# Two accumulators of the first half's projections in one two-bank PSUM tile, in a hybrid HGRN2 and stick-breaking decoder step

## The chip, the core and the metric

One core of one Trainium2 chip runs the whole step as a single program. The metric is the device time of one execution in microseconds (us), the median of several executions. TensorE (PE in the profile) multiplies matrices and writes its sums into PSUM, an accumulator memory of eight banks, each 128 partitions by 512 float32 values. ScalarE (ACT) and VectorE (DVE) read PSUM and do the elementwise work, GpSimd (POOL) gathers cache pages, and the DMA queue of SyncE (SP) brings the weights.

## What is computed

Two layers act on 1024 prompt tokens and on 8 sample tokens, of width 1024. Layer 0 mixes tokens with a gated linear recurrence (HGRN2) beside an attention over 256 memory tokens. After layer 0 one shared K and V is projected. Layer 1 mixes with stick-breaking attention over that K and V, again beside the memory attention. Each layer ends in a SwiGLU block of width 2816. Cut to what matters here:

```python
def swiglu(h, w_gu, w_down):
    gate, up = jnp.split(h @ w_gu, 2, axis=-1)
    return (jax.nn.silu(gate) * up) @ w_down
...
    for l in range(DEPTH):
        g = g_norm[l]
        hn = rmsnorm(h, g[0])
        if l < N_A:
            mix, S = a_mixer(hn, w_in_a[l], lbs[l], hg_norm[l], mem_k[l], mem_v[l], w_o[l], hg_s0[l])
...
        else:
            mix = b_mixer(hn, w_in_b[l - N_A], sb_bias[l - N_A], k_all, v_all, q_pos, k_pos,
                          mem_k[l], mem_v[l], w_o[l])
        h = h + rmsnorm(mix, g[1])
        h = h + rmsnorm(swiglu(rmsnorm(h, g[2]), w_gu[l], w_down[l]), g[3])
        if l == N_A - 1:
            sb_k, sb_v = jnp.split(rmsnorm(h, g_kv) @ w_kv, 2, axis=-1)
```

## The kernel before

**Two halves.** The tokens are cut in two groups that share all weights. Group 0, the first half, is 512 prompt tokens. Group 1, the second half, is the other 512 and the 8 sample tokens, 520 columns. [...]

**A projection.** Every product with a weight matrix goes through `proj` (lines 256 to 268). It makes one accumulator: 128 output features by the group's columns, summed over `nk` blocks of 128 inputs. `split_w` (line 240) loads each 128x512 piece of weights, and ACT (line 250) and DVE (line 251) split it into a high and a low float32r part, so that each block takes three matmuls: high by high, high by low, low by high. With 8 blocks a first-half accumulator has 24 matmuls of 512 columns; in the down projection of the SwiGLU block it has 15 or 12. The split weights stand in five buffers (`wspl`), two of which one 8-block projection fills.

**The accumulator's tile.** `proj` takes a tile `[P, 2, 512]` from the pool `mmp`, which has two buffers, four banks in all. A second-half accumulator fills both banks of its tile. A first-half accumulator writes bank 0 and leaves bank 1 unused (`pv`, line 234, reads `ps[:, 0, :G]`). So two accumulators exist at a time in either half, and the third can start when the reader of the first is done. The other PSUM pools (`smp` with three banks, `nsp` with one) are not touched.

**Readers of the accumulators.** `silu` (line 274) reads its accumulator three times: ACT takes the absolute value (line 277), exponential and logarithm follow (278, 279), DVE takes a minimum and subtracts (280), ACT exponentiates (281), and DVE multiplies by the accumulator (283). The last reader is line 283. In the SwiGLU block (`ffn.part`, line 462) a slice of 128 features is a gate accumulator read by `silu` and an up accumulator read by one DVE multiply (line 472). After 4 or 5 slices the down projection adds 8 accumulators to the residual with one DVE addition each (line 401; a copy on ACT, line 399, in the first part and in `out_proj.mm`, line 411). `heads2` (762), `v_proj` (780), `gate_proj` (791) and `kv_proj` (991) loop over 4 heads, one accumulator per head, read by `silu` or by one ACT copy (942, 785, 799, 997).

**The order.** The stages are generators. `drain` runs them to their end and `weave` (line 222) takes turns between them, so that the recurrence or attention of one half stands beside the SwiGLU parts of the other (lines 1142 to 1193). This sets only the priorities: a scheduler orders the instructions of each engine when the program is built, by its own estimate of when each can run, hands out the buffers of the pools, and writes the semaphores. On the chip each engine then runs its list strictly in that order, and an instruction that waits holds all behind it on its engine.

Of the kernel before, what the change touches and what calls it, by code (L numbers as in the profile page):

```python
# [8 lines left out]
F32 = mybir.dt.float32  # L9
# [8 lines left out]
P = 128  # L18
# [4 lines left out]
def tile_decoder(  # L23
# [8 lines left out]
    ND = D // P  # L32
    NB = x_sample.shape[0]
    NM = mem_prompt.shape[1]
    H = 4
    DFF = w_down.shape[1]
# [3 lines left out]
    G = 512  # L40
    NG = [G, G + NB]
    PW = [G, (G + NB) // 2]
    NPC = [1, 2]
# [3 lines left out]
    def pool(name, bufs, **kw):  # L47
        return ctx.enter_context(tc.tile_pool(name=name, bufs=bufs, **kw))
# [13 lines left out]
    mmp = pool("mmp", 2, space=PSUM)  # L62
# [5 lines left out]
    def nm(s):  # L68
        uid[0] += 1
        return f"{s}_{uid[0]}"  # L70
# [13 lines left out]
    def A(dt=F32):  # L84
        return apool.tile([P, 2, WID], dt, tag="a", name=nm("a"))
# [15 lines left out]
    def C():  # L101
        return cpool.tile([P, 2, 512], F32, tag="c", name=nm("c"))
# [4 lines left out]
    def small(shape, dt=F32, tag="sm", bufs=None):  # L107
        return spool.tile(shape, dt, tag=tag, name=nm(tag), bufs=bufs)
# [39 lines left out]
    for lv in range(7):  # L148
        m = 1 << lv
# [82 lines left out]


    def pv(ps, g):
        return ps[:, 0, :G] if g == 0 else ps[:, :, : PW[1]]

    def sv(ap, g):
        return ap[:, :G] if g == 0 else ap.rearrange("p (a n) -> p a n", a=2)
# [1 line left out]
    def split_w(W, k0, nk, m0):  # L240
        out = []
        for a in range(0, nk, 4):
            n = min(4, nk - a)
            raw = wraw.tile([P, 4, P], F32, tag="w", name=nm("w"))
            nc.sync.dma_start(
                raw[:, :n, :],
                W[(k0 + a) * P : (k0 + a + n) * P, m0 : m0 + P].rearrange("(k p) m -> p k m", p=P),
            )
            ws = wspl.tile([P, 2, 4, P], F32R, tag="ws", name=nm("ws"))
            nc.scalar.copy(ws[:, 0, :n, :], raw[:, :n, :])  # L250
            nc.vector.tensor_sub(ws[:, 1, :n, :], raw[:, :n, :], ws[:, 0, :n, :].bitcast(F32))  # L251
            for i in range(n):
                out.append((ws[:, 0, i, :], ws[:, 1, i, :]))
        return out

    def proj(g, W, k0, nk, m0, xt):
        w = split_w(W, k0, nk, m0)
        ps = mmp.tile([P, 2, 512], F32, tag="mm", name=nm("mm"))
        for k in range(nk):
            wh, wl = w[k]  # L260
            for wi, (wt, xi) in enumerate(((wh, 0), (wh, 1), (wl, 0))):
                for a in range(NPC[g]):
                    o = a * PW[g]
                    nc.tensor.matmul(  # L264
                        ps[:, a, : PW[g]], wt, xt[k][:, xi, o : o + PW[g]],
                        start=(k == 0 and wi == 0), stop=(k == nk - 1 and wi == 2),
                    )
        return ps
# [136 lines left out]
    class out_proj:  # L405


        def __init__(self, g, l, store, last=False):
            self.g, self.l, self.store, self.x, self.last = g, l, store, [], last

        def mm(self, xo, m0=0, m1=ND):
            g = self.g
            if m0 == 0:
                self.R = R_from(self.store)
                self.acc = small([P, WID], tag="st", bufs=3)
            for m in range(m0, m1):
                ps = proj(g, w_o[self.l], 0, ND, m * P, xo)
                evac_raw(g, self.R, ps, m, self.acc, True, True)
                yield

# [36 lines left out]
    class ffn:  # L457
# [4 lines left out]
        def part(self, pi):  # L462
            g, l = self.g, self.l
            n = NG[g]
            f0, nf = PARTS[pi]
            last = pi == len(PARTS) - 1
            mids = []
            for j in range(nf):
                pg = proj(g, w_gu[l], 0, ND, (f0 + j) * P, self.xt)
                sg = silu(None, pg, g)  # L470
                pu = proj(g, w_gu[l], 0, ND, DFF + (f0 + j) * P, self.xt)
                nc.vector.tensor_mul(sv(sg, g), sv(sg, g), pv(pu, g))  # L472
                mt = M(F32R)
                split_to((mt[:, 0, :n], mt[:, 1, :n]), sg[:, :n])
                mids.append(mt)
                yield
            if pi == 0:
                self.R = R_one()
            if last:
                self.acc = small([P, WID], tag="st", bufs=3)  # L480
            for m in range(ND):
                ps = proj(g, w_down[l], f0, nf, m * P, mids)
                evac_raw(g, self.R, ps, m, self.acc, pi == 0, last)
                if last and self.rows:
                    nc.scalar.activation(
                        self.R[m][:, :n], self.R[m][:, :n], AF.Copy, scale=gcol(l, 3, m)
                    )
                    if m == 3:
                        self.first_half()
                if m % 2:  # L490
                    yield
# [268 lines left out]
    carry = const.tile([P, H, P], F32, name="carry")  # L760

    def heads2(g, W, m0, xt, evac, alloc, out):
        for h in range(H):
            if h % 2 == 0:
                out.append(alloc())
            ps = proj(g, W, 0, ND, m0 + h * P, xt)
            evac(out[-1][:, h % 2, :], ps, g)
            yield

# [8 lines left out]
            )  # L778

    def v_proj(g, W, m0, xt, vt, vs):  # L780
        vt.extend((C(), C()) if g else (A(), A()))
        for h in range(H):
            ps = proj(g, W, 0, ND, m0 + h * P, xt)
            t = T()
            nc.scalar.copy(sv(t, g), pv(ps, g))
            to_token(t, vt, h)
            if g:
                nc.vector.tensor_copy(vs[:, h, :], t[:, G : G + NB])
            yield

    def gate_proj(g, W, xt, Ft, Kt):
        n = NG[g]
        for h in range(H):
            if h % 2 == 0:
                Ft.append(A())
                Kt.append(A())
            ps = proj(g, W, 0, ND, 4 * P + h * P, xt)
            f = T()
            nc.scalar.copy(sv(f, g), pv(ps, g))
            e = T()  # L800
            nc.vector.scalar_tensor_tensor(e[:, :n], f[:, :n], -1.0, f[:, :n], op0=ALU.mult, op1=ALU.min)
            nc.scalar.activation(e[:, :n], e[:, :n], AF.Exp)
            nc.scalar.activation(e[:, :n], e[:, :n], AF.Ln, bias=1.0)
            nc.vector.scalar_tensor_tensor(e[:, :n], f[:, :n], 0.0, e[:, :n], op0=ALU.min, op1=ALU.subtract)
            nc.vector.tensor_sub(f[:, :n], e[:, :n], f[:, :n])
            Fd = Ft[-1][:, h % 2, :n]
            Kd = Kt[-1][:, h % 2, :n]
            nc.scalar.activation(Fd, e[:, :n], AF.Exp)
            nc.scalar.activation(Kd, f[:, :n], AF.Exp)
            nc.vector.tensor_scalar(Fd, Fd, oml[:, h : h + 1], lb[:, h : h + 1], op0=ALU.mult, op1=ALU.add)  # L810
            nc.vector.tensor_scalar(Kd, Kd, oml[:, h : h + 1], None, op0=ALU.mult)
            yield
# [176 lines left out]


    def kv_proj(g, xt):
        ks = small([P, 2, H, NB], tag="ks", bufs=1) if g else None
        for j, (out, scr) in enumerate(((sbk_prompt, ksc), (sbv_prompt, vsc))):
            for h in range(H):
                ps = proj(g, w_kv, 0, ND, (j * H + h) * P, xt)
                t = T()
                nc.scalar.copy(sv(t, g), pv(ps, g))
                if g:
                    nc.vector.tensor_copy(ks[:, j, h, :], t[:, G : G + NB])
                pt = S()  # L1000
                for c in range(CH):
                    nc.tensor.transpose(pt[:, c * P : (c + 1) * P], t[:, c * P : (c + 1) * P], ident)
                tok = T()
                nc.vector.tensor_copy(tok[:, :G], pt)
                nc.sync.dma_start(
                    out[0, g * G : (g + 1) * G, h, :].rearrange("(c p) d -> p c d", p=P),
                    tok[:, :G].rearrange("p (c d) -> p c d", d=P),
                )
                nc.sync.dma_start(scr[h][:, g, :], t[:, :G] if j == 0 else tok[:, :G])
                yield  # L1010
        if g:
            for j, dst in enumerate((sbk_sample, sbv_sample)):
                pt = S()
                for h in range(H):
                    nc.tensor.transpose(pt[:NB, h * P : (h + 1) * P], ks[:, j, h, :], ident)
                t = T()
                nc.vector.tensor_copy(t[:NB, :512], pt[:NB, :])
                nc.sync.dma_start(dst.rearrange("b o h d -> (b o) (h d)"), t[:NB, :512])
            yield
# [136 lines left out]
    f0 = ffn(0, 0, o0.x)  # L1156
# [28 lines left out]
    f0 = ffn(0, 1, o0.x)  # L1185
# [40 lines left out]
```

## Time and profile before

| what | us |
|---|---|
| median of three runs | 2559.78 (2555.36 to 2562.91) |
| the profiled execution, its own time | 2560.6 |
| its span in the profile | 2558.9 |
| PE busy in the span | 2525.4 |
| DVE busy | 1556.9 |
| ACT busy | 1218.0 |
| granted PE clock, mean | 0.992 |

By stage, from the view of windows, with the stretches chosen around the first half's SwiGLU parts (times from the start of the span):

| stretch, us | the first half's parts, and what is woven with them | PE busy | DVE busy | ACT busy |
|---|---|---|---|---|
| 404 to 529 | layer 0, part 0, with the second half's recurrence | 124.99 of 125 | 81.51 | 43.79 |
| 640 to 820 | layer 0, end of part 1, parts 2 and 3, with the sample's memory attention | 177.99 of 180 | 120.59 | 75.11 |
| 820 to 900 | layer 0, part 4, nothing woven with it | 80.00 of 80 | 46.30 | 39.43 |
| 1600 to 1830 | layer 1, parts 0 and 1, with stick-breaking attention | 229.75 of 230 | 148.45 | 147.74 |
| 1830 to 2034 | layer 1, end of part 1, parts 2 and 3, with the sample's attention | 195.33 of 204 | 155.75 | 77.00 |
| 2034 to 2165 | second half's output projection, then layer 1, part 4 | 130.81 of 131 | 83.83 | 68.02 |

How to read it: matmuls are pipelined, so one matmul's row is longer than the distance to the next. The mean row of a 512-column matmul is 400 ns, while in an undisturbed run they follow each other every 227 ns. A busy PE row therefore covers small waits too, and a wait shows as idle time only when it outlasts the pipeline.

### The profile page before, as it was taken

What the parts mean: (1) busy time and instruction counts of PE and PEld (TensorE: products, weight loads), DVE (VectorE), ACT (ScalarE), POOL (GpSimd) and SP (SyncE); (2) the same over time, 40 slices, a digit from 0 to 9 for tenths busy, and PEclk for the clock granted to TensorE, in tenths of its full rate; (3) what the DMA queues carried; (4) which work ended last, traced back from release to release, by engine and by line L of the source; (5) the groups of instructions that cost most, each with busy time, mean ns of one, the idle gap of its engine ahead of it and who ended that gap; (6) DMA issues with size and microseconds to landing.
All of it is one profiled execution on the core that took longest, in us unless ns stands there. A gap on an engine that the chain in (4) does not pass through costs nothing.

```text
span 2558.9 us, 40442 instructions
## 1 busy us (share of the span) xinstructions
PE 2525.4 (99%) x15649; PEld 2203.6 (86%) x15649; DVE 1556.9 (61%) x2709; ACT 1218.0 (48%) x2290; POOL 48.8 (2%) x59
## 2 busy tenths in 40 slices
PE   8999999999999999999999999999999999999998
PEld 6888898888777888999999989767776798999998
DVE  6666466654765577555544577666677758444445
ACT  6346543343434445555433455566543245443334
POOL 1000000000000000000000000000041000000000
PEclk9999999999999999999999999999999999999999
DMA  6352242233642445322333445322156444333332
GB/s 186 111 158 71 74 149 81 60 111 112 202 144 87 128 154 178 105 81 63 99 92 93 127 151 180 111 87 67 53 180 211 148 125 124 110 88 101 94 92 68
DMA packets 457707, 297.90 MB, mean 116 GB/s; under 512 B 17573, under 2 KB 422642, under 8 KB 457514
## 3 DMA queue, kind: packets, MB, share of 16 engines
q1 hardware_dynamic: 454954, 286.92, 37.2%
q0 software_dynamic: 2560, 8.39, 1.1%
q8 instruction: 123, 2.02, 0.3%
q14 instruction: 70, 0.57, 0.1%
HBM read 265.44 MB, written 29.80 MB: 115 GB/s over the span
## 4 chain that ended last, share of the span: by engine, by line
issue 25%; PE 23%; DVE 1%; POOL 1%; DMA 0%; ACT 0%; DVEq 0%; POOLq 0%
PE mm L264 22%; POOL c L729 1%; PE s L702 0%; DMA c<-in_cache_sb_k,pidx 0%; DVE ws L251 0%; DVE sc L689 0%; DMA b<-qd 0%; DVE t L280 0%; DMA c<-in_cache_sb_v,pidx 0%; PE s L1123 0%; PE ns L291 0%; PE s L438 0%; DVE yT L540 0%; DVE t L283 0%; DVE c L688 0%
## 5 line engine op out<-in xcount | busy, mean ns | idle before, releaser
L264 PE MATMUL mm<-x,ws 128*128 128x260 f32 (+1 forms) x10080 | 1676.2, 324 | 10.7 <-DVE ws L251 4.2
L264 PEld LDWEIGHTS mm<-x,ws 128*128 128x128 f32 x10080 | 1451.1, 189 | 171.7 <-issue 21.5
L251 DVE TENSOR_TENSOR ws<-w,ws 128x512 fp32r<-128x512 f32 (+1 forms) x800 | 522.5, 657 | 533.5 <-ACT ws L250 522.6
L250 ACT CAST ws<-w 128x512 fp32r<-128x512 f32 (+1 forms) x800 | 474.3, 593 | 694.0 <-PE mm L264 624.1
L264 PE MATMUL mm<-m,ws 128*128 128x260 f32 (+1 forms) x3168 | 543.2, 326 | 1.1 <-DVE r L401 0.6
L264 PEld LDWEIGHTS mm<-m,ws 128*128 128x128 f32 x3168 | 453.8, 188 | 59.9 <-issue 15.0
L277 ACT ACTIVATE t<-mm 128x512 f32<-128x512 f32 (+1 forms) x104 | 62.5, 601 | 195.8 <-PE mm L264 195.7
L401 DVE TENSOR_TENSOR r<-r,mm 128x520 f32<-128x520 f32 (+1 forms) x128 | 88.3, 690 | 97.6 <-PE mm L264 96.5
L472 DVE TENSOR_TENSOR t<-t,mm 128x512 f32<-128x512 f32 (+1 forms) x88 | 60.8, 691 | 72.2 <-PE mm L264 72.1
L280 DVE SCALAR_TENSOR_TENSOR t<-mm,t 128x512 f32<-128x512 f32 (+1 forms) x104 | 72.1, 693 | 43.6 <-ACT t L279 43.4
L281 ACT ACTIVATE t<-t 128x512 f32<-128x512 f32 (+1 forms) x104 | 65.9, 634 | 11.8 <-DVE t L280 11.7
L302 DVE TENSOR_TENSOR st<-st,n 128x512 f32<-128x512 f32 (+1 forms) x98 | 67.0, 690 | 6.5 <-ACT n L301 4.6
L279 ACT ACTIVATE t<-t 128x512 f32<-128x512 f32 (+1 forms) x104 | 66.0, 635 | 2.8
L278 ACT ACTIVATE t<-t 128x512 f32<-128x512 f32 (+1 forms) x104 | 66.2, 637 | 0.0
L283 DVE TENSOR_TENSOR t<-t,mm 128x512 f32<-128x512 f32 (+1 forms) x88 | 60.3, 685 | 5.4 <-ACT t L281 4.8
L271 ACT CAST m<-t 128x512 fp32r<-128x512 f32 (+1 forms) x88 | 54.9, 623 | 18.0 <-DVE t L472 11.3
L272 DVE TENSOR_TENSOR m<-t,m 128x512 fp32r<-128x512 f32 (+1 forms) x88 | 61.0, 693 | 3.9 <-ACT m L271 1.9
L729 POOL DMA_INDIRECT c<-in_cache_sb_k,pidx x16 | 22.7, 1416 | 1869.9 <-DVE r L401 1244.1
L890 PEld LDWEIGHTS s<-a,a 128*128 128x128 f32 x448 | 53.4, 192 | 1.2
L890 PE MATMUL s<-a,a 128*128 128x64 f32 x448 | 53.2, 271 | 0.0
L1025 DVE SCALAR_TENSOR_TENSOR b<-b,b 128x512 f32<-128x512 f32 (+3 forms) x48 | 26.8, 558 | 30.6 <-ACT b L1024 30.1
L641 ACT ACTIVATE b<-s,nmx 128x256 f32<-128x256 f32 x64 | 29.7, 469 | 28.2 <-DVE nmx L635 28.2
(291 smaller groups left out, 1960.9 us busy)
## 6 DMA issues: line engine op xcount, KB each, us to landing
w<-in_w_gu SPq DMA_DIRECT2D x352, 256.0 KB, 2.9
w<-in_w_down SPq DMA_DIRECT2D x160, 256.0 KB, 2.7
w<-in_w_in_a SPq DMA_DIRECT2D x80, 256.0 KB, 3.0
w<-in_w_o SPq DMA_DIRECT2D x64, 256.0 KB, 2.8
w<-in_w_mem_kv SPq DMA_DIRECT2D x32, 256.0 KB, 3.0
c<-in_cache_mem_k SPq DMA_DIRECT2D x16, 512.0 KB, 3.7
c<-in_cache_mem_v SPq DMA_DIRECT2D x16, 512.0 KB, 3.7
w<-in_w_kv SPq DMA_DIRECT2D x32, 256.0 KB, 3.0
```

Of the source, the lines that this page charges most:

```text
L250: nc.scalar.copy(ws[:, 0, :n, :], raw[:, :n, :])
L251: nc.vector.tensor_sub(ws[:, 1, :n, :], raw[:, :n, :], ws[:, 0, :n, :].bitcast(F32))
L264: nc.tensor.matmul(ps[:, a, : PW[g]], wt, xt[k][:, xi, o : o + PW[g]], start=(k == 0 and wi == 0), stop=(k == nk - 1 and wi == 2),)
L272: nc.vector.tensor_sub(dst[1], src, dst[0].bitcast(F32))
L277: nc.scalar.activation(av, pv(ps, g), AF.Abs)
L278: nc.scalar.activation(av, av, AF.Exp, scale=-1.0)
L279: nc.scalar.activation(av, av, AF.Ln, bias=1.0)
L280: nc.vector.scalar_tensor_tensor(av, pv(ps, g), 0.0, av, op0=ALU.min, op1=ALU.subtract)
L281: nc.scalar.activation(av, av, AF.Exp)
L302: nc.vector.tensor_add(acc[:, :n], acc[:, :n], t[:, :n])
L401: nc.vector.tensor_add(dst, dst, pv(ps, g))
L890: nc.tensor.matmul(plv[:, hh, c, :], K_[:, hh, cs], rhs, start=True, stop=True)
```

## The change

In the first half, two successive accumulators of one stage are given the two banks of one tile. A new helper `banks` holds what is left of a tile; each stage makes one (`bk`) and hands it to `proj`. In the first half `next()` gives bank 0 of a new tile, then bank 1 of the same tile, then a new tile. In the second half it gives a whole tile, as before. Neighbours that share a tile are the gate and the up accumulator of a SwiGLU slice, down projections `m` and `m + 1`, heads 0 and 1, and heads 2 and 3. The matmuls, their operands, the loads and the readers stay as they are; the pool keeps its two buffers.

```diff
     def pv(ps, g):
-        return ps[:, 0, :G] if g == 0 else ps[:, :, : PW[1]]
+        return ps if NPC[g] == 1 else ps[:, :, : PW[g]]
+
+    class banks:
+
+
+        def __init__(self, g):
+            self.g, self.left = g, []
+
+        def next(self):
+            if not self.left:
+                t = mmp.tile([P, 2, 512], F32, tag="mm", name=nm("mm"))
+                self.left = [t] if NPC[self.g] == 2 else [t[:, 0, :], t[:, 1, :]]
+            return self.left.pop(0)
...
-    def proj(g, W, k0, nk, m0, xt):
+    def proj(g, W, k0, nk, m0, xt, bk):
         w = split_w(W, k0, nk, m0)
-        ps = mmp.tile([P, 2, 512], F32, tag="mm", name=nm("mm"))
+        ps = bk.next()
...
-                        ps[:, a, : PW[g]], wt, xt[k][:, xi, o : o + PW[g]],
+                        ps[:, a, : PW[g]] if NPC[g] == 2 else ps, wt, xt[k][:, xi, o : o + PW[g]],
...
             mids = []
+            bk = banks(g)
             for j in range(nf):
-                pg = proj(g, w_gu[l], 0, ND, (f0 + j) * P, self.xt)
+                pg = proj(g, w_gu[l], 0, ND, (f0 + j) * P, self.xt, bk)
                 sg = silu(None, pg, g)
-                pu = proj(g, w_gu[l], 0, ND, DFF + (f0 + j) * P, self.xt)
+                pu = proj(g, w_gu[l], 0, ND, DFF + (f0 + j) * P, self.xt, bk)
...
             for m in range(ND):
-                ps = proj(g, w_down[l], f0, nf, m * P, mids)
+                ps = proj(g, w_down[l], f0, nf, m * P, mids, bk)
```

`out_proj.mm`, `heads2`, `v_proj`, `gate_proj` and `kv_proj` each get the same two edits: `bk = banks(g)` ahead of the loop, and `bk` as `proj`'s last argument.

More of the change, by code (lines that the diff above doesn't have):

```diff
@@ L415, in mm @@
                 self.acc = small([P, WID], tag="st", bufs=3)
+            bk = banks(g)
             for m in range(m0, m1):
-                ps = proj(g, w_o[self.l], 0, ND, m * P, xo)
+                ps = proj(g, w_o[self.l], 0, ND, m * P, xo, bk)
                 evac_raw(g, self.R, ps, m, self.acc, True, True)
@@ L467, in part @@
             mids = []
+            bk = banks(g)
             for j in range(nf):
-                pg = proj(g, w_gu[l], 0, ND, (f0 + j) * P, self.xt)
+                pg = proj(g, w_gu[l], 0, ND, (f0 + j) * P, self.xt, bk)
                 sg = silu(None, pg, g)
-                pu = proj(g, w_gu[l], 0, ND, DFF + (f0 + j) * P, self.xt)
+                pu = proj(g, w_gu[l], 0, ND, DFF + (f0 + j) * P, self.xt, bk)
                 nc.vector.tensor_mul(sv(sg, g), sv(sg, g), pv(pu, g))
@@ L762, in heads2 @@
     def heads2(g, W, m0, xt, evac, alloc, out):
+        bk = banks(g)
         for h in range(H):
@@ L765, in heads2 @@
                 out.append(alloc())
-            ps = proj(g, W, 0, ND, m0 + h * P, xt)
+            ps = proj(g, W, 0, ND, m0 + h * P, xt, bk)
             evac(out[-1][:, h % 2, :], ps, g)
@@ L780, in v_proj @@
     def v_proj(g, W, m0, xt, vt, vs):
+        bk = banks(g)
         vt.extend((C(), C()) if g else (A(), A()))
         for h in range(H):
-            ps = proj(g, W, 0, ND, m0 + h * P, xt)
+            ps = proj(g, W, 0, ND, m0 + h * P, xt, bk)
             t = T()
@@ L791, in gate_proj @@
     def gate_proj(g, W, xt, Ft, Kt):
+        bk = banks(g)
         n = NG[g]
@@ L796, in gate_proj @@
                 Kt.append(A())
-            ps = proj(g, W, 0, ND, 4 * P + h * P, xt)
+            ps = proj(g, W, 0, ND, 4 * P + h * P, xt, bk)
             f = T()
@@ L991, in kv_proj @@
     def kv_proj(g, xt):
+        bk = banks(g)
         ks = small([P, 2, H, NB], tag="ks", bufs=1) if g else None
@@ L994, in kv_proj @@
             for h in range(H):
-                ps = proj(g, w_kv, 0, ND, (j * H + h) * P, xt)
+                ps = proj(g, w_kv, 0, ND, (j * H + h) * P, xt, bk)
                 t = T()
```

## The prediction

> **What bounds the kernel now.** I read the page first, then the matmul groups with their shapes kept apart, PE's waits, and stretches of the timeline.
>
> ```profile
> PE 2525.4 (99%) x15649; PEld 2203.6 (86%) x15649; DVE 1556.9 (61%) x2709; ACT 1218.0 (48%) x2290; POOL 48.8 (2%) x59
> ...
> L264 PE MATMUL mm<-x,ws 128*128 128x512 f32 x3360 | 829.2, 400 | 10.3 <-DVE ws L251 4.2 <-DVE t L283 3.1 <-DVE t L472 1.8
> L264 PE MATMUL mm<-m,ws 128*128 128x512 f32 x1056 | 275.9, 407 | 1.1 <-DVE r L401 0.6 <-ACT ws L250 0.4
> ...
> PE mm L264 <- DVE ws L251: 4.2, 2, 2.7
> PE mm L264 <- DVE t L283: 3.4, 6, 1.1
> PE mm L264 <- DVE t L472: 1.8, 2, 1.1
> PE mm L264 <- DVE r L401: 0.6, 1, 0.6
> PE mm L264 <- ACT ws L250: 0.4, 1, 0.4
> ```
>
> PE is busy 99% of the span, so PE's list sets the time, and only what PE waits for can change it. The edit touches 3360 + 1056 = 4416 first-half matmuls, in 3360/24 = 140 eight-block accumulators and 80 down accumulators. All the waits recorded ahead of them are 10.3 + 1.1 = 11.4 us; waits for a reader to free a tile are 3.4 + 1.8 + 0.6 = 5.8 us. So this edit has at most about 11 us to win, 0.4% of the time, and no such bound on what it can lose.
>
> How late a reader is, in a quiet stage (layer 0, part 4), in a loaded one (layer 1, stick-breaking), and a release:
>
> ```profile
> 834.85 0.60 ACT L277 ACTIVATE t<-mm 128x512 f32<-128x512 f32 x1 [2.10 <-PE mm L264]
> ...
> 838.83 0.68 DVE L283 TENSOR_TENSOR t<-t,mm 128x512 f32<-128x512 f32 x1
> ...
> 840.29 0.69 DVE L472 TENSOR_TENSOR t<-t,mm 128x512 f32<-128x512 f32 x1 [0.77 <-PE mm L264]
> ...
> 1745.63 0.59 ACT L277 ACTIVATE t<-mm 128x512 f32<-128x512 f32 x1
> ...
> 1751.84 0.68 DVE L283 TENSOR_TENSOR t<-t,mm 128x512 f32<-128x512 f32 x1
> ...
> 1968.64 0.68 DVE L283 TENSOR_TENSOR t<-t,mm 128x512 f32<-128x512 f32 x1
> ...
> 1969.38 3.01 PE L264 MATMUL mm<-x,ws 128*128 128x512 f32 x12 [1.15 <-DVE t L283]
> ```
>
> From the gate's first reader at 834.85 to the up accumulator's at 840.29 lie 5.44 us, 24 matmuls: one every 227 ns. A matmul's row is 400 ns, so a result is there 0.17 us after its 227 ns are over, and the reader starts some 0.03 us later. Counted from the end of the accumulator's matmul time, the silu chain has let go after 0.2 + (839.51 - 834.85) = 4.86 us, a DVE read (add, up multiply) after 0.2 + 0.69 = 0.89, an ACT copy after 0.2 + 0.6 = 0.8. PE goes on 0.05 us after a release (1969.32 to 1969.38). In the loaded stage the same chain takes 0.2 + 6.89 = 7.1 us.
>
> **The change, part by part.** Nothing is added to any engine: the order of the two built programs has the same 13,248 projection matmuls, the same readers, and the same loads, 38 of SP's 1053 rows in another place. Moved are PE's order and its waits. The 220 first-half tiles become 111. But the semaphores are kept by tile: of the 109 second-bank accumulators 103 now wait, at their first matmul, for the last reader of the first bank, though it is another bank. In a slice the up accumulator waits for line 283 of its own gate. The scheduler therefore fills in between with the next tile's accumulator, puts it aside, and comes back: resumed accumulators go from 22 to 110.
>
> What decides is how much matmul time stands, in PE's order, between the end of an accumulator and the first matmul that waits for its reader. Before, that is mostly a whole accumulator of the other tile: 24 x 0.227 = 5.44 us against 4.91, or 12 x 0.227 = 2.72 against 0.94. After, it is what the scheduler could find. The costliest case is the last slice of a SwiGLU part. In layer 0, part 4, the last gate ends, 2 of its matmuls after the previous up; 9 down matmuls follow (9 x 0.227 = 2.04 us); then its up waits for the silu, 4.91 - 2.04 = 2.87 us, of which 0.49 falls earlier, on a down accumulator that starts 0.45 us after the up multiply's accumulator instead of 0.94.
>
> I did this for every reader wait of the first half. A shortfall is lateness plus 0.05 less the matmul time between, with earlier shortfalls inside the interval taken off. "Quiet" takes the lateness above for all; "own" takes for each reader the lateness that it has in the trace before.
>
> | reader | waits | short, quiet | us, quiet | short, own | us, own |
> |---|---|---|---|---|---|
> | silu, line 283 | 51 | 19 | 24.7 | 27 | 37.4 |
> | up multiply, 472 | 30 | 10 | 4.7 | 11 | 5.6 |
> | additions, 401 | 54 | 12 | 1.8 | 19 | 6.4 |
> | copies, 399, 799, 942 | 24 | 11 | 3.2 | 12 | 4.5 |
> | sum | 159 | 52 | 34.4 | 69 | 53.9 |
>
> Nine silu waits make 22.4 of the quiet 24.7 us: 4.0 between the recurrence's query heads and the first value head (0.87 us of PE work between), 4.5 at the second slice of layer 1, part 2 (0.45 us between), and 1.7 to 2.4 at the last slices of five parts and at two more slices of layer 1, part 3. The same working on the program before gives 7.3 us by own lateness, where the rows show 5.8. So the net is 34.4 - 7.3 = 27.1 at the low end and 53.9 - 7.3 = 46.6 at the high end. The own lateness belongs to the same stages and comes nearest to the trace's own waits, but each PE wait lets DVE and ACT catch up, so I take +38.
>
> The clock adds a little:
>
> ```profile
> 1898.00:1908.00 10.00, 7.38 (x22) 5.85 (x23) 10.00 (x13) 0.62 (x1) 9.09 (x4) 0.66 0.69 194
> 535.00:545.00 10.00, 10.00 (x35) 8.18 (x36) 4.33 (x5) 3.32 (x6) 0.00 (x0) 0.72 0.30 87
> ```
>
> These are windows; after the engines comes the granted clock. With PE idle for 2.6 of 10 us the clock was 0.66, worth 3.4 us; in the second it dropped to 0.72 with PE busy throughout, so waits are not its only cause. Three waits above (4.0, 3.6 and 5.5 us with own lateness) are longer; one lies where the first window is already. Bounds 0 and 3 x 3.4 = 10; I take 3, because the long row at 0.66 is one that exists already.
>
> [...]
>
> The sum, on the profiled execution's own 2560.6 us (0.8 above the median): 2560.6 + 38 + 3 - 0.8 = 2601 us.
>
> **The rivals.**
>
> *Free banks, faster.* Four accumulators in flight let PE always find work: a second bank would not wait for the first one's reader, and the 11.4 us of waits would go; 2560 - 11 = 2549. For it: 220 tiles become 111 while the pool keeps four banks. Against it: the 103 waits in the built order. It decides only if the readers prove much earlier than their rows, by 3 us for silu. Chance 0.07.
>
> [...]
>
> *Hidden, no change.* The new waits could fall where PE waits anyway (8.7 us of PE idle between 1830 and 2034), and the old 5.8 us go. That hides 14.5 of 34.4 at most, which leaves 20; for no change DVE and ACT would have to catch up besides, by half of it. Chance 0.05, at 2560 to 2567.
>
> *A ring of waits, slower still.* An accumulator put aside keeps its split weights, up to two of five buffers, so the splits on ACT (line 250, which already waits 624 us for PE) stop earlier, and readers queue behind them. If one split (0.6 us on ACT, 0.69 on DVE) came late behind each of the 69 short waits and half of these showed, 35 x 0.6 = 21 us more: 2622, with the high clock bound 2629. For it: 110 resumed accumulators. Against it: ACT is 48% busy, and weights cost PE only 4.2 + 0.4 us now. Chance 0.18.
>
> **How the numbers follow.** My forecast, waits of +27 to +47 with clock of 0 to 10, has chance 0.70 and its own range 2587 to 2617. The range for 8 in 10 leaves out the faster rival and the tail of the ring: 2567 to 2628. What a measurement can tell from no change is 0.3%, 7.7 us: faster 0.07, within 0.05, slower 0.88.
>
> **What would show it.** Right: PE's row for line 264's 512-column forms gets idle time of 25 us or more ahead of it, released by line 283's successor first; the timeline of layer 0, part 4 shows PE standing about 2.4 us at the last up accumulator; the second half's part alone (2307 to 2531) takes the same time. Wrong: first-bank readers and second-bank matmuls overlapping, PE's waits for readers at or below 6 us, or the loss on waits for split weights (the ring).

## The result, and the profile after

| | median, us | runs |
|---|---|---|
| before | 2559.87 | 2555.36 to 2563.33, 6 runs |
| with the change | 2601.84 | 2593.53 to 2607.17, 6 runs |

The ratio is 1.016, with a 95% interval of 1.0137 to 1.0184: the change costs 42 us, against a forecast of 2601 us, 41 more than before. The profiled execution has a span of 2605.2 us, 46.3 more than the one of before. Ratios compare fast executions alone: one execution of a control below, the kernel before with a copy, took 9139.92 us at a granted clock of 0.371 and is left out of its ratio.

The groups of matmuls of the changed kernel, shapes kept apart (count, busy us and mean ns, then the idle time ahead of them and what ended it); the code has moved by 12 to 14 lines: line 276 is the matmul of before's line 264, 295 is 283, 413 is 401 and 486 is 472:

```profile
L276 PE MATMUL mm<-x,ws 128*128 128x512 f32 x3360 | 835.1, 403 | 28.7 <-DVE t L295 16.9 <-DVE a L295 4.4 <-DVE t L486 3.4
L276 PE MATMUL mm<-m,ws 128*128 128x512 f32 x1056 | 283.2, 411 | 7.3 <-DVE r L413 4.2 <-DVE t L486 2.6 <-ACT ws L262 0.4
```

The idle time ahead of the first half's matmuls went from 11.4 to 36.0 us. Their busy time rose too, by 5.9 + 7.3 = 13.2 us, with the same matmuls: short waits, and a clock of 0.989 against 0.992 before, hide in rows that overlap (a row is 403 ns in the mean, with 227 ns from one start to the next in an undisturbed run). Together that is 37.8 us; the other 8.5 us of the longer span lie in the other groups of matmuls. PE's waits name the readers:

```profile
PE mm L276 <- DVE t L295: 18.7, 9, 5.5
PE mm L276 <- DVE t L486: 6.0, 8, 2.6
...
PE mm L276 <- DVE a L295: 4.4, 1, 4.4
PE mm L276 <- DVE r L413: 4.2, 2, 3.5
...
PE mm L276 <- DVE ws L263: 1.9, 1, 1.9
```

Before, the rows for the readers were 3.4, 1.8 and 0.6 us, and the one for split weights was 4.2. Readers took all of the increase, split weights fell.

The place that the prediction worked through, the last slice of layer 0, part 4, in the changed kernel's timeline (start, duration, engine and line; idle time in brackets):

```profile
876.70 0.59 ACT L289 ACTIVATE t<-mm 128x512 f32<-128x512 f32 x1
...
877.00 2.32 PE L276 MATMUL mm<-m,ws 128*128 128x512 f32 x9 [0.42 <-DVE t L486]
...
880.86 0.69 DVE L295 TENSOR_TENSOR t<-t,mm 128x512 f32<-128x512 f32 x1 [0.70 <-ACT t L293]
...
881.61 2.56 PE L276 MATMUL mm<-x,ws 128*128 128x512 f32 x10 [2.28 <-DVE t L295]
```

The last gate's silu starts at 876.70. PE does nine down matmuls and then stands for 2.28 us, until silu's last multiply ends at 881.55, before the up accumulator's first matmul, which writes to the neighbouring bank. The second half's accumulators keep a tile each. Its last long stretch in the chain of work that ended last, first before and then after:

```profile
2307.14 224.17 PE mm L264 x1872
```

```profile
2353.47 224.18 PE mm L276 x1872
```

The same 1872 matmuls take the same time; they only start 46.3 us later.

### The profile page after: what moved, and what is told of

Read it like the earlier page. It is cut to its first block, busy times and chain, and to the rows that moved or that the text cites. A ratio compares the mean times of both kernels' runs of the same rounds, so it can differ in the third digit from the quotient of the medians.

```text
span 2605.2 us, 40413 instructions
## 1 busy us (share of the span) xinstructions
PE 2540.8 (98%) x15649; PEld 2206.4 (85%) x15649; DVE 1554.2 (60%) x2709; ACT 1214.8 (47%) x2290; POOL 49.8 (2%) x59
## 4 chain that ended last, share of the span: by engine, by line
PE 45%; DVE 2%; issue 1%; DMA 1%; ACT 1%; POOL 0%; POOLq 0%; DVEq 0%; SPq 0%; ACTq 0%
PE mm L276 40%; PE s L1079 1%; PE s L1091 1%; PE s L1064 1%; POOL c L743 0%; DVE c L702 0%; DMA b<-qd 0%; PE s L716 0%; DVE sc L703 0%; PE s L675 0%; PE s L644 0%; DVE ws L263 0%; PE ns L303 0%; DMA c<-in_cache_sb_v,pidx 0%; PE s L668 0%
## 5 line engine op out<-in xcount | busy, mean ns | idle before, releaser
L276 PE MATMUL mm<-m,ws 128*128 128x260 f32 (+1 forms) x3168 | 550.4, 327 | 7.4 <-DVE r L413 4.2
L293 ACT ACTIVATE t<-t 128x512 f32<-128x512 f32 (+1 forms) x104 | 65.7, 634 | 20.8 <-DVE t L292 20.5
L295 DVE TENSOR_TENSOR t<-t,mm 128x512 f32<-128x512 f32 (+1 forms) x88 | 60.6, 689 | 10.1 <-ACT t L293 9.4
```

The lines of the kernel that those rows point to most:

```text
L276: nc.tensor.matmul(ps[:, a, : PW[g]] if NPC[g] == 2 else ps, wt, xt[k][:, xi, o : o + PW[g]], start=(k == 0 and wi == 0), stop=(k == nk - ...
L293: nc.scalar.activation(av, av, AF.Exp)
```

## The experiments

All are judged by the median beside runs of before on the same chip, and by the ratio with its interval.

**Only the slices share a tile.** `banks` gets a flag, and only `ffn.part`'s slices keep pairs (`NPC[g]`, the matmuls that a group's columns take, is 1 in the first half and 2 in the second):

```diff
+            self.g, self.left, self.pair = g, [], pair
...
-                self.left = [t] if NPC[self.g] == 2 else [t[:, 0, :], t[:, 1, :]]
+                self.left = [t] if NPC[self.g] == 2 else ([t[:, 0, :], t[:, 1, :]] if self.pair else [t[:, 0, :]])
...
+            bk = banks(g, False)
             for m in range(ND):
```

> Only gate and up of a slice share a tile; down, heads, key/value and output projections keep a tile each. Theory (a second bank waits for the last reader of the first): 43 of the 103 same-tile waits stay, those on silu; from the trace after the change they are worth 21 us, plus 3 to 6 on the up multiply, less the 4 us that slices already waited before: 2575 to 2585, the largest of the three parts. Rival (any reordering of PE costs about the same, wherever the pairs are): each part alone loses about 40, 2600. Rival (weights held by accumulators put aside): waits for split weights above 10 us.

Measured: 2583.12 us against 2561.28, ratio 1.0085 (1.0068 to 1.0102), +21.8 us. The groups of this kernel:

```profile
L276 PE MATMUL mm<-x,ws 128*128 128x512 f32 x3360 | 828.6, 401 | 21.7 <-DVE t L295 15.5 <-DVE t L486 3.1 <-DVE ws L263 1.7
L276 PE MATMUL mm<-m,ws 128*128 128x512 f32 x1056 | 274.7, 406 | 3.3 <-DVE t L486 2.2 <-DVE r L413 0.6 <-ACT ws L262 0.4
```

The wait for silu is there with the slices alone, and split weights cost 1.7 + 0.4 us, less than the 4.2 + 0.4 of before. Half of the loss lies here.

**Only the down projections share a tile.** The same flag, set for the loop over `m` alone.

> Only down projections m and m + 1 share a tile. Theory: 40 same-tile waits, on one DVE addition or ACT copy of 0.9 us each; from the trace after the change 7 us, less 1 to 2 that were there before: 2563 to 2570. Rival (any reordering): 2600.

Measured: 2561.47 us against 2561.28, ratio 1.0005 (0.9994 to 1.0016), so anything from 1.5 us won to 4 us lost, where 2 to 9 us were expected. The down projections of this kernel:

```profile
L276 PE MATMUL mm<-m,ws 128*128 128x512 f32 x1056 | 282.1, 410 | 3.0 <-DVE r L413 2.6 <-ACT ws L262 0.4
```

The down pairs' waits are there: the idle time ahead of the same matmuls was 1.1 us before and is 7.3 with the whole change, and all that PE waits for the addition comes to 3.2 us here, 0.6 before and 4.2 with the whole change. The time hardly shows it; the idle time ahead of the other first-half projections is 6.0 us here, 10.3 before.

**Only heads, key/value and output projections share tiles.**

> Only heads, key/value and output projections share tiles. Theory: 19 same-tile waits, on one ACT copy, but also the silu of the recurrence's query heads, 4.5 us in one place; from the trace after the change 7 to 8 us: 2563 to 2570. Rival (any reordering): 2600.

Measured: 2574.49 us against 2561.28, ratio 1.0056 (1.0041 to 1.0072), +13.2 us, more than expected. PE's wait between the recurrence's query heads is there (4.4 us for line 295), and the waits for readers, counted below, rise by 8.5 us. Most of the rest can be the clock: its mean over the six executions is 0.9920, over those of before beside them 0.9934, an estimate of 4 us of 2560. The three parts add up to 21.8 + 0.2 + 13.2 = 35 us of 42. That no part alone costs near 40 rules out that any reordering of PE is dear, wherever it is.

**Both projections of a pair ahead of the first read.** If a second bank waits because the reader of the first is written ahead of it, the reader can be written behind both. The slice as an example; the other loops likewise, in the first half alone:

```diff
                 pg = proj(g, w_gu[l], 0, ND, (f0 + j) * P, self.xt, bk)
+                pu = proj(g, w_gu[l], 0, ND, DFF + (f0 + j) * P, self.xt, bk) if g == 0 else None
                 sg = silu(None, pg, g)
-                pu = proj(g, w_gu[l], 0, ND, DFF + (f0 + j) * P, self.xt, bk)
+                if g:
+                    pu = proj(g, w_gu[l], 0, ND, DFF + (f0 + j) * P, self.xt, bk)
```

> The change with all its pairs, but in the first half both projections of a pair are written ahead of the first reader. Theory: no second bank waits for a reader any more (0 same-tile waits in the built order); the readers wait for the second bank instead, up to 5.4 us later, but the other tile then covers them with 10.9 us of matmuls against 4.9 us of silu, so PE's waits for readers fall below the 8 us of before: 2550 to 2562. Rival (two accumulators in one tile are slow in themselves, or a tile freed late starves PE): 2595 or more.

Measured: 2609.59 us against 2561.28, ratio 1.0184 (1.0168 to 1.0201). The expectation failed, and the rival's number came. (The mean granted clock is 0.986 here and 0.993 in the runs of before beside it, so by estimate up to 20 of these 48 us are the clock's.) The built order did what it should: no second bank waits for a reader. But the readers now wait for the second bank, by tile as well, and that moves the lateness elsewhere. The timeline of this kernel in two places, the last slice of layer 0, part 2, and layer 1, part 2:

```profile
706.05 2.25 PE L276 MATMUL mm<-m,ws 128*128 128x512 f32 x9
706.25 0.60 ACT L296 ACTIVATE t<-mm 128x512 f32<-128x512 f32 x1 [2.10 <-PE mm L276]
...
713.17 0.68 DVE L496 TENSOR_TENSOR t<-t,mm 128x512 f32<-128x512 f32 x1
...
713.91 2.30 PE L276 MATMUL mm<-m,ws 128*128 128x512 f32 x4 [5.61 <-DVE t L496]
```

```profile
1925.08 0.59 ACT L296 ACTIVATE t<-mm 128x512 f32<-128x512 f32 x1
...
1932.55 0.68 DVE L302 TENSOR_TENSOR t<-t,mm 128x512 f32<-128x512 f32 x1
1933.14 0.68 DVE L263 TENSOR_TENSOR ws<-w,ws 128x512 fp32r<-128x512 f32 x1
...
1933.88 2.50 PE L276 MATMUL mm<-x,ws 128*128 128x512 f32 x5 [8.47 <-DVE ws L263]
```

In the first, silu starts only when gate and up are both there; nine down matmuls later nothing is left, and PE stands 5.6 us, until the tile comes free. In the second, a weight split that PE needs stands on DVE behind the multiply of a silu that began late, among the sample's cache work, and PE stands 8.5 us. The rival named two causes. That sharing a tile is slow in itself is not what these rows show. That a tile freed late starves PE is what the first place shows. The expectation had left out the end of a part, where too little work is left to cover a silu, and DVE's order.

**The same for the slices alone**, all else with a tile each:

> Only slices share a tile, and in the first half gate and up are both multiplied ahead of the first reader; all else has a tile each, as before. Theory (what was lost with all pairs before their reads is silu starting 5.4 us later: at the last slice of a part nothing covers it, and in the loaded stages weight splits queue behind it on DVE): 2590 to 2610, above the 2583 of shared slices in the old order. Rival (that loss sat in the heads and down projections): 2560 to 2575.

Measured: 2584.22 us against 2561.62, ratio 1.0088 (1.0066 to 1.011): below the range expected and above the rival's, and the same as slices shared in the old order. Of the 48 us of all pairs, 23 belong to the slices. The other half came with heads, down and output projections, and was not taken apart.

**An early release, pairs kept.** In `silu`, the first half copies the accumulator and goes on from the copy:

```diff
         a = T()
         av = sv(a, g)
+        if g == 0:
+            c = T()
+            nc.scalar.copy(c[:, :G], pv(ps, g))
+            ps = c[:, :G]
         nc.scalar.activation(av, pv(ps, g), AF.Abs)
```

> The change, and in the first half ACT first copies the accumulator that silu reads to SBUF; silu then reads the copy. The bank is free after one copy (0.85 us) and no longer after 4.9 us; all 103 same-tile waits stay, and 52 copies of 0.6 us are added on ACT. Theory (what costs is how late the reader of the first bank lets go): the 26 us that PE waits for silu in the trace after the change fall to 5 or less, and some of the half-clock stretches with them: 2570 to 2582. Rival (the new order of PE, or the sharing of a tile as such): the loss stays, 2598 or more.

Measured: 2563.14 us against 2561.61, ratio 1.0013 (1.0 to 1.0025). Some 40 of the 42 us are back, more than expected, with every pair and all 103 waits in place. A part of that is the clock: its mean is 0.9949 over these executions and 0.9932 over those of before beside them, an estimate of 4 us. The groups of this kernel:

```profile
L276 PE MATMUL mm<-x,ws 128*128 128x512 f32 x3360 | 826.9, 399 | 8.2 <-DVE ws L263 2.7 <-DVE t L490 2.1 <-ACT t L291 1.6
L276 PE MATMUL mm<-m,ws 128*128 128x512 f32 x1056 | 277.4, 406 | 1.9 <-DVE r L417 1.5 <-ACT ws L262 0.4
```

Idle time is 10.1 us, against 36.0 with the change and 11.4 before, and line 291 here is the copy: 1.6 us in place of 21.3 for silu's multiply. What decides is, for the most part, when the first bank's reader lets go, not that two accumulators share a tile.

**The copy in the kernel before**, as a control: the same edit without pairs.

> The kernel before, with the copy ahead of silu in the first half: what the copies cost by themselves, and what an early release is worth without the pairs. Theory: the waits for silu in the trace before (about 4 us) go, 52 copies on ACT lie beside PE: 2554 to 2563. Rival (the copies cost time on their own): 2570 or more, and then the time of the run with pairs and copies has to be read against this one.

Measured: 2557.58 us against 2561.61, ratio 0.998 (0.997 to 0.999). The 52 copies cost no time and are worth 0.2%. Beside this kernel, on the same chip, the one with pairs and copies is some 6 us slower (2563.14 against 2557.58): so much the pairs still cost with the early release, against 42 us without it. What those 6 us are was not taken apart.

**Four tiles of one bank.** `mmp` gets four buffers of `[P, 512]`; `proj` takes one in the first half, two in the second (`PW[g]` is 512 columns for each in the first half, 260 in the second), and each reader runs once per bank. The memory's key and value projections, which had two banks of one tile, take two tiles:

```diff
-    mmp = pool("mmp", 2, space=PSUM)
+    mmp = pool("mmp", 4, space=PSUM)
...
-        ps = mmp.tile([P, 2, 512], F32, tag="mm", name=nm("mm"))
+        ps = [MM()[:, : PW[g]] for _ in range(NPC[g])]
...
-                        ps[:, a, : PW[g]], wt, xt[k][:, xi, o : o + PW[g]],
+                        ps[a], wt, xt[k][:, xi, o : o + PW[g]],
```

> Four tiles of one bank in place of two of two. A first-half accumulator takes one tile, a second-half accumulator two, read by two instructions of 260 columns each. So the first half may have four accumulators in flight, as the change wants, but none waits for the reader of its neighbour. Theory: only waits for a tile to come free are left, 44 in the built order against 136 before, and PE waits for readers under 4 us: 2548 to 2562; the doubled reads of the second half lie on ACT and DVE, off PE's path. Rival (four accumulators in flight disturb PE's order or the weights): 2580 or more.

Measured: 2558.7 us against 2561.61, ratio 0.9988 (0.9978 to 0.9998). The groups of this kernel:

```profile
L267 PE MATMUL mm<-x,ws 128*128 128x512 f32 x3360 | 826.1, 399 | 9.8 <-DVE ws L254 8.8 <-ACT x L359 0.8 <-DVE t L289 0.2
L267 PE MATMUL mm<-m,ws 128*128 128x512 f32 x1056 | 276.1, 407 | 0.5 <-DVE r L408 0.3 <-ACT m L274 0.3
```

Four accumulators in flight, from the same four banks, leave 0.5 us of idle time behind readers (line 289 is silu's multiply, 408 the addition). The second bank's wait is gone, as the faster rival had it, and the gain is small because there was little to win: 3 us of the 5.8, with waits for split weights up to 8.8.

**Both together**, four single banks and the copy:

> Four single-bank tiles and, in the first half, the copy ahead of silu. Theory: both took the first half's waits for readers to about 1 to 9 us by themselves, and what is left in either trace are other waits (split weights, start, end), so together they add little: 2552 to 2560. Rival (their gains add up in full, 3 + 4 us): 2554 or less with an interval that excludes either alone.

Measured: 2556.98 us against 2561.62, ratio 0.9983 (0.9971 to 0.9994). It has the lowest median of all, but its interval overlaps with either alone. The simplest of the three is the kernel before with the copy.

## Why the prediction was right

For its steps, the waits were counted in the trace, each first-half projection matmul set against the program's order: how much longer than the usual 226 to 230 ns the distance was ahead of a first matmul that waits for a reader. Columns two and three are the prediction's quiet and own ends. Such a count depends on what is called usual: with a usual distance for each shape, the sums of the last two columns are 7.7 and 39.8.

| reader | quiet | own | before | after |
|---|---|---|---|---|
| silu | 24.7 | 37.4 | 4.6 | 24.5 |
| up multiply | 4.7 | 5.6 | 2.2 | 8.8 |
| additions | 1.8 | 6.4 | 1.2 | 6.5 |
| copies | 3.2 | 4.5 | 0 | 3.4 |
| sum | 34.4 | 53.9 | 8.0 | 43.2 |

*What bounds the kernel.* Right: PE's list sets the time. Freed of all reader waits, with four single banks, the kernel gains 3 us, well inside the bound of 11.

*The mechanism.* Right, and shown: the cost is the second bank's wait for the first bank's reader. With the wait left and the reader early, the loss is 1.5 us against before, or 6 against the kernel before with the same copy; with four accumulators that share nothing there is none. The term was +38, taken between 27 and 47; measured are 43.2 - 8.0 = 35.2 us, or 32 by the other count. (The prediction's 22 and 110 count how often an accumulator is resumed; the accumulators that are resumed number 10 and 83.)

*The kinds.* Silu came out at the quiet end, not the own end, probably because DVE and ACT catch up while PE stands; no run tests that. The up multiply was mis-sized, 8.8 us where 5.6 was the high end. Most of the excess is one wait, in layer 1, part 2. The changed kernel's PE there, and then its DVE:

```profile
1913.70 2.88 PE L276 MATMUL mm<-x,ws 128*128 128x512 f32 x12
1919.14 0.70 PE L276 MATMUL mm<-x,ws 128*128 128x512 f32 x2 [2.56 <-DVE t L486]
1925.37 2.92 PE L276 MATMUL mm<-x,ws 128*128 128x512 f32 x6 [5.53 <-DVE t L295]
```

```profile
1913.71 1.23 DVE L702 TENSOR_TENSOR c<-c,b 128x1024 f32<-128x1024 f32 x1 [3.69 <-DMA b<-qd]
1916.05 1.23 DVE L702 TENSOR_TENSOR c<-c,b 128x1024 f32<-128x1024 f32 x1 [1.11 <-DMA b<-qd]
1917.19 1.22 DVE L703 TENSOR_REDUCE sc<-c 128x8 f32<-128x1024 f32 x1
1918.32 0.68 DVE L486 TENSOR_TENSOR t<-t,mm 128x512 f32<-128x512 f32 x1
```

The up multiply stands in DVE's list behind the sample's scores, and those wait 3.69 and 1.11 us for a DMA. PE stood 2.56 us for it, and 5.53 us two matmuls later for silu, where the prediction had 5.5 with own lateness. A lateness taken from the old trace doesn't hold where the new order puts a DMA's wait ahead of the reader.

*The clock.* The term of +3 was too small, inside its bounds of 0 and 10. Up to the last 8 us of the span, the granted clock is at half, 0.50, for 51.2 us, against 30.7 before, so by estimate up to 10.2 us are lost where 3 were put. These windows of the changed kernel show it (after the engines, the granted clock):

```profile
1920.00:1930.00 10.00, 4.63 (x14) 3.69 (x15) 10.00 (x13) 2.57 (x6) 7.42 (x7) 0.66 0.55 165
1978.00:1988.00 10.00, 7.13 (x17) 4.47 (x18) 6.43 (x10) 0.62 (x1) 0.00 (x0) 0.66 0.58 177
2165.00:2175.00 10.00, 7.69 (x23) 5.80 (x22) 2.75 (x4) 2.99 (x7) 0.00 (x0) 0.66 0.54 167
60.00:70.00 10.00, 6.51 (x19) 5.01 (x19) 4.73 (x9) 4.77 (x10) 0.00 (x0) 0.66 0.21 54
```

Each holds one of the new waits, PE is idle for 2.3 to 5.4 of the 10 us, and the clock is at half for 6.8 us. In the run with the early release the mean clock of the profiled execution is 0.996, against 0.989 with the change and 0.992 before. The executions of the changed kernel differ by the clock too: two at 0.993 took 2593.5 and 2594.3 us, two at 0.989 took 2607.0 and 2607.2.

The waits and the clock together, 35.2 + 10.2 = 45.4, come near the 46.3 us between the two profiled spans, in part by chance. Where half clock falls on a stretch in which PE stands, as in the first window, where PE is busy for 4.63 of the 10 us, it has less work to slow; and outside the first half's projections PE's idle time grew by 6 us, which neither term counts. That the forecast hit the median so closely is luck in part: the waits were put 3 us too high and the clock 7 too low, and the profiled run is some 5 us above its kernel's median.

*The rivals.* Free banks: refuted for this program by the 103 waits. In the program with four single tiles the waits for readers do go, but it wins 3 us, not 11. Hidden: refuted, since the window with idle PE, layer 1, part 2, took the largest new waits on top: PE's idle time, 8.7 us there before, is 18.8 between 1840 and 2060 us of the changed kernel. The ring: refuted, since waits for split weights fell from 4.2 to 1.9 us.

## What to carry to other kernels

Where a framework keeps its semaphores by tile, two accumulators that share a tile are one buffer: the second waits for the last reader of the first, as 103 of 109 do here in the built order, and the slow chain of readers on the first cost most: silu, 24.5 of the 43.2 us of waits. Give each accumulator its own tile, or release it with one copy, which here left 6 of the 42 us. And before a wait is called cheap, count how much work stands in the built order between the releaser's input and the waiter, and compare it with the reader's time from the trace.

## What was not expected of the hardware

The granted clock fell beside waits of quite different lengths. In the trace with the change it is 0.50 for 6.8 us from 2167 us on, after a distance of 2.79 us from one matmul's start to the next, and for 3.4 us from 713 us on, after one of 1.72 us. Distances of 2.67 and 2.64 us, at 879 and 2002 us, were followed by no drop. In the trace before, the drop in the prediction's first window, 6.8 us from 1899 us on, has 3.07 us from start to start ahead of it. Three drops between 530 and 625 us, 20.5 us in all, are in the trace before and in the one after, at somewhat different places, with PE busy and no distance above 0.6 us in the 12 us ahead of any of them. What decides whether a drop follows a wait, and what caused those three, is not shown by these traces.
